# A skipped block of no-operations ahead of three engines' programs, in a sum of reciprocals on one core

## The chip, the cores and the metric

The kernel runs on one core of a Trainium2 chip. The time is the device time of one execution in microseconds (us). The core has five engines with a program each: TensorE (PE, matrix multiply), VectorE (DVE), ScalarE (ACT), GpSimd (POOL) and SyncE (SP, which here issues all DMAs). The engines meet only at semaphores. Sixteen DMA engines move data between the chip's memory (DRAM) and the on-chip memory.

## The reference

```python
def setup_inputs():
    batch, seq, dim = 32, 512, 1024
    return {"x": np.abs(np.random.randn(batch, seq, dim)).astype(np.float32) + 1e-6}

def reference(x):
    return np.sum(1.0 / x, axis=-1).astype(np.float32)
```

The input has 32 x 512 rows of 1024 float32 numbers, 67.1 MB. Of each row the sum of the reciprocals is wanted, 16,384 numbers in all.

## The kernel before

The 16,384 rows lie as 128 partitions of 128 rows each. "Row r" in the kernel means row r of every partition, a tile of 128 x 1024. The last two rows (126 and 127) are worked in two halves each, as rows 126 to 129 of the plan.

Per row the kernel avoids 1024 divisions by pairing the first half a with the second half b: 1/a + 1/b = (a + b) / (a * b). The product a * b goes through ScalarE, which takes its logarithm (scaled by 2^17) and then the exponential of the negative logarithm, so that 1/(a * b) comes out. VectorE multiplies by a + b and sums up in the same instruction, or multiplies a row's both halves by the same reciprocal of the product, which needs no a + b.

The order of all work is written out by hand in the string PLAN (lines 43 to 73), and the same order holds on each engine. A token is a letter, a row, "+n" for n rows at once and "@b" for a place:

- D: SyncE loads the next n rows into `ring`, a buffer of 40 rows (line 187). There are 33 loads, from 7168 KB down to 256 KB. A load waits until the rows that it overwrites are done with.
- P: POOL makes the products a * b of a row into `prod` (line 199). W and V: VectorE makes them (line 220); for V, TensorE has first copied b into a PSUM bank (C, a multiplication by the identity matrix, line 209), for W both halves are read from `ring`.
- S: TensorE forms a + b in a PSUM bank with two multiplications by the identity (line 232).
- L and E: ScalarE's logarithm (line 242) and exponential (line 251). E writes to a PSUM bank where it has an "@".
- R: VectorE's multiplication and sum (line 267), which fills one column of `sums`.
- When the first 114 rows are done, their sums leave in six DMAs (line 289); the rest leaves in one DMA at the end (line 291).

The helper `note` keeps a history of who reads and writes which space (a row of the ring, a slot of `prod`, a PSUM bank). The framework adds a semaphore wait for every dependency that it sees. Where another wait of the same engine already implies a dependency, `note` declares it away with `tc.declare_no_dep`. In the kernel before, a dependency on an earlier instruction of the same engine is passed over ahead of that step:

```python
        for other in needed:
            o_inst, o_engine, o_tick, _, _, o_known = other
            if o_engine == engine:
                continue
            if o_tick <= known.get(o_engine, 0):
                tc.declare_no_dep(inst, o_inst, reason="implied by other waits")
                continue
```

At the head of the programs ScalarE loads its table of functions (line 84) and POOL makes the identity matrix `ident` by `make_identity` (a fill and a select of another file, masks.py:197 and 199). TensorE's first multiplication reads it.

Of the kernel before, what the change touches and what calls it, by code (L numbers as in the profile page):

```python
# [8 lines left out]


@with_exitstack
def kernel(
# [5 lines left out]
    nc = tc.nc  # L18
    f32 = mybir.dt.float32
    P = 128  # L20
# [3 lines left out]
    R = 40  # L24
    NP = 22
    LAST = F - 2
    DONE = 114
    S = float(2**17)

    PLAN = """
        D2 D10 D14 D14 P0+2 C3@3 S2@0 V3 P2 L0+2@0 C11@3 S3@1 E0+2@6 P4+2 V11 L2+2@2 R0 S6@2
        E2+2 R1 P6+2 L4+2@4 R2 R3 E4+2@6 S7@0 P8+2 L6+2@8 R4 S10@1 E6+2 R5 P10 L8+2@10 R6 R7  # L40
        S11@2 E8+2@6 L10+2@6 R8 E10+2 R9 D11 R10 R11 P12+2 C19@3 S14@0 V19 P14+2 L12+2@12
        S15@1 E12+2@6 S18@2 R12 P16+2 L14+2@16 R13 E14+2 R14 P18 L16+2@18 R15 S19@0 E16+2@6
        P20+2 L18+2@14 R16 S22@1 E18+2 R17 D9 P22+2 L20+2@20 R18 R19 E20+2@6 S23@2 P24+2
        L22+2@0 R20 E22+2 R21 L24+2@2 R22 R23 E24+2@6 P26 C27@3 R24 S26@0 P28+2 V27 R25 D7
        L26+2@4 C35@3 E26+2 S27@1 P30+2 V35 L28+2@8 R26 S30@2 R27 E28+2@6 P32+2 L30+2@10 R28
        S31@0 E30+2 R29 P34 L32+2@12 S34@1 R30 R31 E32+2@6 P36+2 S35@0 L34+2@6 R32 E34+2 R33
        D7 P38+2 S38@2 L36+2@16 R34 R35 E36+2@6 S39@1 P40+2 L38+2@18 R36 C43@3 E38+2 R37 D6
        S42@0 P42 L40+2@14 V43 R38 E40+2@6 P44+2 R39 S43@2 L42+2@20 R40 E42+2 S46@1 R41 D3
        P46+2 L44+2@0 R42 R43 E44+2@6 S47@0 P48+2 L46+2@2 R44 S50@2 E46+2 R45 P50 L48+2@4
        R46 C51@3 R47 E48+2@6 S51@1 P52+2 V51 R48 D6 L50+2@8 C59@3 E50+2 R49 P54+2 S54@0  # L50
        L52+2@10 V59 R50 E52+2@6 R51 S55@2 P56+2 L54+2@12 R52 E54+2 S58@1 R53 D5 P58
        L56+2@16 R54 R55 E56+2@6 S59@0 P60+2 L58+2@6 R56 S62@2 E58+2 R57 D4 P62+2 L60+2@14
        R58 R59 E60+2@6 S63@1 P64+2 L62+2@18 R60 S66@0 E62+2 R61 D4 P66 L64+2@20 R62 C67@3
        R63 E64+2@6 P68+2 S67@2 V67 R64 L66+2@0 S70@1 R65 D4 E66+2 P70+2 L68+2@2 R66 R67
        S71@0 E68+2@6 P72+2 L70+2@4 R68 D3 E70+2 R69 D2 C75@3 P74 L72+2@10 S74@2 R70 V75
        P76+2 E72+2@6 R71 S75@1 L74+2@8 R72 D2 E74+2 R73 D2 P80 S78@0 L76+2@12 R74 P81
        L80@16 R75 S79@2 E76+2@6 P78+2 L81@17 R76 D2 S81@1 E80@5 E81 R80 L78+2@6 W82 E78+2
        R81 R77 D1 D1 D1 D1 D1 P88 C85@6 S85@1 R78 P83 L88@18 V85 E88@7 R79 P84 S84@0
        L82+2@14 R88 E82+2@5 P86+2 L84+2@19 R82 D1 E84+2 R83 D1 D1 D1 C90@7 P91 L86+2@0
        S91@2 R85 P93 V90 E86+2@5 R84 P92 S90@1 L90+2@2 R87 L93@21 W89 L92@10 R86 D1 D1 D1  # L60
        D1 E93@7 P94 S97@0 E92@6 R93 E90+2 P97 S94@3 L89@11 R92 E89@7 P95 L97@8 R91 S95@4
        E97 R90 L94+2@4 W96 R97 P101 C99@6 L96@9 R89 E94+2 S100@0 P98 V99 E96@5 L101@12 R95
        P100 S99@1 L98@13 R96 E101@7 L99+2@16 R101 E98@6 P104 C103@5 R94 E99+2 S105@2 R98
        P102 L104@18 V103 E104@7 W105 L102+2@6 R100 P107+2 C106@6 L105@14 R104 E102+2@4
        S108@0 V106 E105 R102 L106+3@19 P109 S107@3 R103 P110 E106+3 R105 S106@4 R99 P111+2
        L109+2@0 R107 S112@1 R108 E109+2@6 R106 L111+2@10 P114 R109 S111@0 E111+2 R110 P113
        L114@15 R111 C115@7 P116 L113@2 R112 E114@6 V115 E113@5 S117@0 P117 R114 L116@3
        L115@8 P118 E116@7 R113 S118@1 E115@6 P119 L117+2@12 R116 E117+2 R115 P120 S120@2
        L119@9 R117 P121 L120@4 S121@3 R118 E119@7 E120 R119 P122 L121@5 S122@0 E121 R120
        P123 L122@18 R121 E122 W124 L123@6 R122 L124@7 W125 S125@1 E123@7 E124@6 R123 P126  # L70
        L125@14 P127 L126@16 S127@0 R124 E125 P128 L127@17 S128@2 E126@7 P129 R125 E127
        S129@3 L128@19 R126 L129@20 E128 R127 E129 R128 R129
    """.split()

    Ln = mybir.ActivationFunctionType.Ln
# [4 lines left out]
    x_v = x.flatten_outer_dims().rearrange("(p f) d -> p f d", p=P)  # L80
    out_v = out.flatten().rearrange("(p f) -> p f", p=P)

    act_sets = list(get_activation_tables(nc.m.arch).keys())
    nc.scalar.add_instruction(  # L84
        mybir.InstLoadActFuncSet(
            name=nc.get_next_instruction_name(),
            act_func_set_id=act_sets.index("natural_log_exp_and_others"),
            ins=[],
            outs=[],
        )  # L90
    )

    pool = ctx.enter_context(tc.tile_pool(name="pool", bufs=1))
    pspool = ctx.enter_context(
        tc.tile_pool(name="pspool", bufs=1, space=bass.MemoryType.PSUM)
# [1 line left out]
    ring = pool.tile([P, R, D], f32)  # L97
# [1 line left out]
    sums = pool.tile([P, F], f32)  # L99
    ident = pool.tile([P, P], f32)  # L100
    ps = pspool.tile([P, 8, H], f32)
    make_identity(nc, ident)

    def parse(tok):
        body, _, b = tok[1:].partition("@")
        r, _, n = body.partition("+")
        return tok[0], int(r), int(n or 1), int(b) if b else None

    ops = [parse(tok) for tok in PLAN]

    pslot = {r + j: b + j for op, r, n, b in ops if op == "L" for j in range(n)}

    def place(r):
        if r < LAST:
# [9 lines left out]
    left = set(range(DONE))  # L124
    bank, copied, halves, summed = {}, {}, set(), set()

    history = {}
    begun = {}
    count = {}

    def note(engine, inst, reads=(), writes=()):
        inst = inst.ins
        known = dict(begun.get(engine, {}))
        before = {}
        for spaces, writing in ((reads, False), (writes, True)):
            for space in spaces:  # L140
                for other in history.get(space, ()):
                    if writing or other[3]:
                        before[other[0].name] = other
        needed = sorted(before.values(), key=lambda o: -o[4])
        for other in needed:
            o_inst, o_engine, o_tick, _, _, o_known = other
            if o_engine == engine:
                continue
            if o_tick <= known.get(o_engine, 0):
                tc.declare_no_dep(inst, o_inst, reason="implied by other waits")  # L150
                continue
            for e, t in o_known.items():
                known[e] = max(known.get(e, 0), t)
            known[o_engine] = max(known.get(o_engine, 0), o_tick)
        count[engine] = count.get(engine, 0) + 1
        begun[engine] = known
        entry = (engine, count[engine])
        if engine == "SP":
            entry = (f"load {count[engine]}", 1)
        for spaces, writing in ((reads, False), (writes, True)):  # L160
            for space in spaces:
                history.setdefault(space, []).append(
                    (inst, *entry, writing, sum(count.values()), known)
                )

    def rows(r, n, h=None):
        spaces = []
# [7 lines left out]
    def slots(r, n):  # L175
        return [("slot", pslot[q]) for q in range(r, r + n)]

    with tc.manual_schedule():
        for op, r, n, b in ops:
            p = pslot.get(r)  # L180
            if op == "D":
                n, r = r, loaded
                while n:
                    q, at, w = place(r)
                    a = q % R
                    m = min(n, R - a, LAST - r) if r < LAST else 1
                    inst = nc.sync.dma_start(  # L187
                        out=ring[:, a : a + m, at : at + 2 * w],
                        in_=x_v[:, q : q + m, at : at + 2 * w],
                    )  # L190
                    note("SP", inst, writes=rows(r, m))
                    r, n = r + m, n - m
                loaded = r
# [34 lines left out]
            elif op == "S":  # L228
                bank[r] = b
                halves.add(r)  # L230
                for h in range(2):
                    inst = nc.tensor.matmul(  # L232
                        ps[:, b, : place(r)[2]],
                        lhsT=ident,
                        rhs=xs(r, h),
                        start=h == 0,
                        stop=h == 1,
                    )
                    note("PE", inst, rows(r, 1, h), [("bank", b)])
            elif op == "L":  # L240
                pg = prod[:, p : p + n, : place(r)[2]]
                inst = nc.scalar.activation(out=pg, in_=pg, func=Ln, scale=S)  # L242
# [1 line left out]
            elif op == "E":  # L244
# [5 lines left out]
                        bank[r + j] = b + j  # L250
                inst = nc.scalar.activation(out=rc, in_=pg, func=Exp, scale=-1.0)  # L251
                if b is None:
                    note("ACT", inst, writes=slots(r, n))
                else:
                    banks = [("bank", b + j) for j in range(n)]
                    note("ACT", inst, slots(r, n), banks)
            elif op == "R":
                q, at, w = place(r)
                other = ps[:, bank[r], :w]
# [2 lines left out]
                else:  # L262
# [16 lines left out]
                    "DVE",  # L279
                    inst,  # L280
                    [("bank", bank[r])],
                    slots(r, 1) if r in halves else rows(r, 1),
                )

                left.discard(r)
                if not left:
                    for c in range(0, DONE, DONE // 6):
                        part = slice(c, min(c + DONE // 6, DONE))
                        nc.sync.dma_start(out=out_v[:, part], in_=sums[:, part])
                    left.add(-1)  # L290
        nc.sync.dma_start(out=out_v[:, DONE:], in_=sums[:, DONE:])


# [28 lines left out]
```

## Time and profile before

| | us |
|---|---|
| three runs | 168.47, 168.10, 167.86 |
| their median | 168.1 |
| span of the profiled execution, first to last instruction | 166.3 |
| SyncE issues the first load | 0.74 |
| first data packet | 1.75 |
| load 0 has landed | 5.6 |
| ScalarE's first logarithm starts | 8.03 |
| TensorE's and VectorE's first work starts | 17.8 and 19.9 |
| last load has landed | 161.3 |
| VectorE's last instruction ends | 164.0 |
| last output has landed | 165.5 |

The span is that of the profiled execution; the runs that were timed are others. A profile names a line, the engine, the operation, and what is written from what ("prod<-ring"). Busy times of the engines overlap. The share of DMA is that of the 16 DMA engines together. A load has landed when all 16 engines have reported the end of their part. "Instruction" among the DMA queues is the fetching of program code; those packets run on the same 16 DMA engines.

### The profile page before, as it was taken

How to read it: one execution, taken by the hardware profiler on the slowest of the kernel's cores; microseconds unless marked ns; L12 is line 12 of the kernel's file. 1: busy time of each engine (PE TensorE's matmuls, PEld its weight loads, DVE VectorE, ACT ScalarE, POOL GpSimd, SP SyncE). 2: the span in 40 equal slices, each digit the busy share in tenths (PEclk: the TensorE clock that was granted, in tenths of full speed). 3: DMA queues.
4: the chain of work that ended last, by engine and by line, in shares of the span. 5: the costliest groups of instructions: out<-in, count | busy, mean ns of one | idle time of the engine just before them, and what ended most of it. 6: DMA issues, size and time to landing. Idle time of an engine off the chain costs nothing.

```text
span 166.3 us, 1348 instructions
## 1 busy us (share of the span) xinstructions
PE 132.5 (80%) x292; PEld 55.2 (33%) x292; DVE 128.3 (77%) x282; ACT 132.3 (80%) x157; POOL 128.2 (77%) x81
## 2 busy tenths in 40 slices
PE   0000799978855999999999999988699979989982
PEld 0000333333312444444343433324234424433351
DVE  0000119885787699898998898989899999999994
ACT  3040073949995899999799999996999999999992
POOL 1500795069995999999999999948977869999860
PEclk9999999999996999999999999999999999999999
DMA  5999999999998989999999999999999999999940
GB/s 189 536 394 394 441 441 441 441 441 441 441 441 349 509 368 446 430 417 438 441 434 434 406 426 446 429 424 424 414 437 437 414 410 428 410 409 410 400 139 4
DMA packets 5768, 67.26 MB, mean 404 GB/s; under 512 B 1536, under 2 KB 1536, under 8 KB 3200
## 3 DMA queue, kind: packets, MB, share of 16 engines
q1 hardware_dynamic: 5760, 67.18, 95.6%
q8 instruction: 2, 0.03, 0.1%
q14 instruction: 6, 0.05, 0.1%
HBM read 67.11 MB, written 0.07 MB: 404 GB/s over the span
## 4 chain that ended last, share of the span: by engine, by line
DMA 57%; PE 18%; ACT 8%; DVE 6%; POOL 6%; issue 3%; SPq 1%; ACTq 0%; POOLq 0%; DVEq 0%
DMA ring<-in_x_dram 57%; PE ps L232 15%; POOL prod L199 6%; ACT prod L242 4%; PE ps L209 3%; ACT ps L251 2%; DVE ring L267 2%; DVE prod L267 2%; ACT prod L251 2%; DVE prod L220 1%; SPq L187 1%; DVE sums L267 0%; ACTq L242 0%; POOLq L199 0%; DVEq L317 0%
## 5 line engine op out<-in xcount | busy, mean ns | idle before, releaser
L199 POOL TENSOR_TENSOR prod<-ring 128x1024 f32<-128x1024 f32 (+2 forms) x75 | 127.5, 1727 | 33.5 <-DMA ring<-in_x_dram 27.1
L232 PE MATMUL ps<-ring,ident 128*128 128x512 f32 (+1 forms) x260 | 116.9, 596 | 5.2 <-DVE sums L267 4.5
L242 ACT ACTIVATE prod<-prod 128x1024 f32<-128x1024 f32 (+2 forms) x78 | 68.5, 892 | 24.9 <-DVE prod L220 14.3
L267 DVE CUSTOM_DVE_ANT_1 ring<-ring,ps 128x1024 f32<-128x1024 f32 (+1 forms) x65 | 76.4, 1208 | 8.9 <-ACT ps L251 8.7
L232 PEld LDWEIGHTS ps<-ring,ident 128*128 128x128 f32 x260 | 49.2, 193 | 71.7 <-issue 51.6
L267 DVE CUSTOM_DVE_ANT_0 prod<-prod,ps 128x512 f32<-128x512 f32 (+1 forms) x63 | 40.9, 677 | 0.4 <-PE ps L232 0.4
L209 PE MATMUL ps<-ring,ident 128*128 128x512 f32 x32 | 19.3, 689 | 25.7 <-DMA ring<-in_x_dram 24.0
L251 ACT ACTIVATE ps<-prod 128x1024 f32<-128x1024 f32 (+2 forms) x41 | 34.1, 838 | 4.5 <-DVE sums L267 3.7
L251 ACT ACTIVATE prod<-prod 128x1024 f32<-128x1024 f32 (+3 forms) x37 | 34.4, 931 | 0.9
L220 DVE TENSOR_TENSOR prod<-ring,ps 128x512 f32<-128x512 f32 x16 | 10.9, 684 | 26.3 <-PE ps L209 26.3
L209 PEld LDWEIGHTS ps<-ring,ident 128*128 128x128 f32 x32 | 6.0, 213 | 36.0 <-issue 21.4
L267 DVE DVE_READ_ACCUMULATOR2_ANT sums<- 128x1 f32 x130 | 10.7, 82 | 0.0
L220 DVE TENSOR_TENSOR prod<-ring 128x512 f32<-128x512 f32 x6 | 4.1, 688 | 0.1
L84 ACT ACT_TABLE_LOAD x1 | 1.3, 1283 | 0.7 <-PEq L306 0.7
L267 DVE CUSTOM_DVE_ANT_0 prod<-prod,ps,sums 128x256 f32<-128x256 f32 x2 | 0.9, 475 | 0.0
masks.py:197 POOL MEMSET ident<- 128x128 f32 x1 | 0.2, 204 | 0.3 <-POOLq L306 0.3
masks.py:199 POOL TENSOR_SCALAR_AFFINE_SELECT ident<-ident 128x128 f32<-128x128 f32 x1 | 0.3, 292 | 0.1
L306 POOL MEMSET const-float32-0.0<- 128x1 f32 x1 | 0.1, 98 | 0.2 <-issue 0.2
L306 POOL MEMSET const-bfloat16-1.0<- 128x1 bf16 x1 | 0.1, 101 | 0.0
L306 POOL MEMSET const-uint8-127<- 128x1 uint8 x1 | 0.1, 101 | 0.0
L306 POOL MEMSET const-float32-1.0<- 128x1 f32 x1 | 0.1, 98 | 0.0
## 6 DMA issues: line engine op xcount, KB each, us to landing
ring<-in_x_dram SPq DMA_DIRECT2D x2, 7168.0 KB, 41.2
ring<-in_x_dram SPq DMA_DIRECT2D x2, 3584.0 KB, 29.3
ring<-in_x_dram SPq DMA_DIRECT2D x2, 3072.0 KB, 31.9
ring<-in_x_dram SPq DMA_DIRECT2D x3, 2048.0 KB, 34.0
ring<-in_x_dram SPq DMA_DIRECT2D x1, 5632.0 KB, 30.3
ring<-in_x_dram SPq DMA_DIRECT2D x5, 1024.0 KB, 31.8
ring<-in_x_dram SPq DMA_DIRECT2D x1, 5120.0 KB, 16.5
ring<-in_x_dram SPq DMA_DIRECT2D x1, 4608.0 KB, 30.7
```

What stands on the lines that cost most here:

```text
L84: nc.scalar.add_instruction(mybir.InstLoadActFuncSet(name=nc.get_next_instruction_name(), act_func_set_id=act_sets.index("natural_log_exp_ ...
L187: inst = nc.sync.dma_start(out=ring[:, a : a + m, at : at + 2 * w], in_=x_v[:, q : q + m, at : at + 2 * w],)
L199: inst = nc.gpsimd.tensor_tensor(out=prod[:, p : p + m, :w], in0=ring[:, a : a + m, at : at + w], in1=ring[:, a : a + m, at + w : at + 2 * w],
L209: inst = nc.tensor.matmul(ps[:, b, : place(r)[2]], lhsT=ident, rhs=xs(r, 1), start=True, stop=True,)
L220: inst = nc.vector.tensor_tensor(out=prod[:, p, :w], in0=xs(r, 0), in1=in1, op=mult)
L232: inst = nc.tensor.matmul(ps[:, b, : place(r)[2]], lhsT=ident, rhs=xs(r, h), start=h == 0, stop=h == 1,)
L242: inst = nc.scalar.activation(out=pg, in_=pg, func=Ln, scale=S)
L251: inst = nc.scalar.activation(out=rc, in_=pg, func=Exp, scale=-1.0)
L267: inst = nc.vector.tensor_tensor_reduce(out=row, in0=row, in1=other, scale=S, scalar=total if q in summed else 0.0, op0=mult, op1=add, acc ...
L306: nc = _bacc.Bacc("TRN2", target_bir_lowering=False, num_devices=1)
```

## The change

Three things change.

First, ahead of the work of TensorE, VectorE and ScalarE there now stands a section that sets a register to 0 and runs 176, 56 or 48 no-operations if it equals 1. It does not, so a branch goes past them. The section is a critical one, as the framework calls it: the three stand one after the other, VectorE's waits for TensorE's and ScalarE's for VectorE's. All five programs are thereby cut into more blocks, with a branch from each to the next: SyncE and POOL have three more branches each. ScalarE's table load, POOL's fill of the identity and the first load are put behind the sections in their own engines' order; they wait for no semaphore for that.

Second, `note` now looks at same-engine dependencies too, so that those implied by other waits are declared away. The built program has 28 semaphore instructions in VectorE's body instead of 42, and 21 in POOL's instead of 33. R's entry in `note` also names the column of `sums` that it writes.

Third, the identity matrix is made by the same two POOL instructions in the kernel itself, instead of by the helper.

The tokens of PLAN are the same 497 in the same order, and each engine's instructions stand in the same order. New letters A and Z, and a mark "!", are understood but not used.

```diff
+    PADS = (('tensor', 176), ('vector', 56), ('scalar', 48))
...
         for other in needed:
             o_inst, o_engine, o_tick, _, _, o_known = other
-            if o_engine == engine:
-                continue
             if o_tick <= known.get(o_engine, 0):
                 tc.declare_no_dep(inst, o_inst, reason="implied by other waits")
+                continue
+            if o_engine == engine:
                 continue
...
+    skips = []
+    for engine, pad in PADS:
+        engine = getattr(nc, engine)
+        with tc.tile_critical() as skip:
+            zero = engine.to_reg(0)
+            with engine.If_eq(zero, 1):
+                for _ in range(pad):
+                    engine.nop(hint="idle", nofuse=True)
+        skips.append(skip)
+
+    def behind(inst):
+        for skip in skips:
+            tc.add_manual_dep(
+                inst.ins,
+                skip.name,
+                mybir.DependencyInfo(
+                    mybir.DependencyClass.NoSync,
+                    mybir.DependencyReason.SCHED_ONLY,
+                ),
+            )
+
+    act_sets = list(get_activation_tables(nc.m.arch).keys())
+    table = nc.scalar.add_instruction(
...
+    behind(table)
 
     with tc.manual_schedule():
-        for op, r, n, b in ops:
+        behind(nc.gpsimd.memset(ident, 0.0))
+        nc.gpsimd.affine_select(
+            out=ident,
+            in_=ident,
...
+        for op, r, n, b, held in ops:
...
+                    if r == 0:
+                        behind(inst)
                     note("SP", inst, writes=rows(r, m))
...
-                    slots(r, 1) if r in halves else rows(r, 1),
+                    (slots(r, 1) if r in halves else rows(r, 1)) + [("sum", q)],
```

## The prediction

> **What bounds the kernel now.** I read the page first, then the chain of waits, then the DMA queues by window, then the timelines of ScalarE and VectorE near the landings that they wait for.
>
> ```profile
> span 166.3 us, 1348 instructions
> PE 132.5 (80%) x292; PEld 55.2 (33%) x292; DVE 128.3 (77%) x282; ACT 132.3 (80%) x157; POOL 128.2 (77%) x81
> DMA  5999999999998989999999999999999999999940
> q1 hardware_dynamic: 5760, 67.18, 95.6%
> q8 instruction: 2, 0.03, 0.1%
> q14 instruction: 6, 0.05, 0.1%
> ...
> DMA 57%; PE 18%; ACT 8%; DVE 6%; POOL 6%; issue 3%; SPq 1%; ACTq 0%; POOLq 0%; DVEq 0%
> ```
>
> The 16 DMA engines are full from the second slice to the 38th, and the chain that ended last is DMA for 57%. Cut into 2 us pieces, the packets of the data queue cover 0.98 to 1.04 of 16 engines from 2 to 158 us: the input stream never pauses. Each load is cut evenly over the 16 engines (8 partitions each), so a load has landed when its slowest engine is through, and whatever else one engine carries makes it late for good. The two lines "instruction" are such extra work: the fetching of program code, 2 packets of 16 KB and 6 of 8 KB.
>
> The trace's landing events show what they cost. Load 3 (the fourth) ends on all 16 engines within 0.38 us (51.18 to 51.56). Then a code packet of 8 KB starts at 52.42, and load 4's last engine is 0.94 behind its first; after the 16 KB packet at 69.64, load 5 shows 1.63; after 8 KB at 78.18 a third engine stands at 0.69; after 8 KB at 109.44 and 111.23, load 10 has 1.97 (110.75 to 112.72); after 16 KB at 140.84 a further engine stands at 1.7. At load 28 (156.65 to 158.67) the spread is 2.03, with engines at 2.03, 1.79, 1.70, 0.78, 0.76 and the other eleven under 0.39. In the packet records a fetch takes its own 0.3 us (8 KB) or 1.0 to 1.1 us (16 KB), and the data packet behind it on the same engine is longer by 0.36 to 0.66: 0.95 us each for the fetches at 52.42 and 111.23, 0.7 for those at 78.18 and 109.44, 1.5 for the 16 KB ones. The fetches at 52.42 and 111.23 hit the same DMA engine (a packet ends on it 4 ns after each starts, the next nearest is 10 ns off or more), the two of 16 KB two different ones.
>
> Who waits for the late engine is in the timelines (start, us, instruction, and the idle time before it with its releaser), of ScalarE and then of VectorE:
>
> ```profile
> 111.76 1.06 ACT L251 ACTIVATE prod<-prod 128x1024 f32<-128x1024 f32 x1
> 114.16 0.63 ACT L242 ACTIVATE prod<-prod 128x512 f32<-128x512 f32 x1 [1.34 <-POOL prod L199]
> ...
> 157.37 0.69 DVE L220 TENSOR_TENSOR prod<-ring 128x512 f32<-128x512 f32 x1
> 157.97 0.68 DVE L267 CUSTOM_DVE_ANT_0 prod<-prod,ps 128x512 f32<-128x512 f32 x1
> 158.58 0.08 DVE L267 DVE_READ_ACCUMULATOR2_ANT sums<- 128x1 f32 x1
> 158.69 0.69 DVE L220 TENSOR_TENSOR prod<-ring 128x512 f32<-128x512 f32 x1
> ```
>
> ScalarE's 1.34 us end with a POOL product that waited for load 10 (112.72). VectorE's W124 and W125 start 0.02 us after loads 27 and 28 have landed (157.34, 158.67); from W125 on VectorE has no gap to its last instruction at 164.0, and 2.3 us of output and end barrier follow. So the end hangs on the slowest DMA engine's landing of loads 27 and 28, with VectorE close behind: between 142 and 158.7 it idles only 0.6 us in all.
>
> **The change part by part.** *Head.* TensorE, VectorE and ScalarE run their branch one after the other (each waits for the one before), SyncE and POOL pass 3 more branches each, and the first load is issued behind SyncE's. No trace row is a lone branch. SyncE's gap from a semaphore row to its DMA is 0.066 us over one branch (0.671 to 0.737) and 0.047 without (35.080 to 35.127): one costs 0.02, and at most the whole 0.066. Three: 0.06 to 0.2; I take 0.1, as the measured difference is the nearer row. It is on the path, since the stream never pauses. The Trainium skill (Advanced Engine Details and Errata, Control Flow Timing) gives about 51 ns for a branch, 0.15 us for three; no row here shows a branch alone. ScalarE's table load (1.28 us, now at 0.73) comes after all three sections. Each has some 10 instructions outside the no-ops, by the sequencer rows of 17 to 51 ns at most 0.5 us each, so it ends by 3.6; ScalarE first works at 8.03. If that cover went, ScalarE's first pair (2.1 us) could still start at 18.5, since it then sits idle 10.53 us until 20.68. TensorE and VectorE first work at 17.8 and 19.9. Cost 0.1.
>
> *Waits removed.* Same-engine waits that others imply: 14 semaphore instructions less on VectorE, 12 on POOL. VectorE's take 0.021 us each, and in the trace the instruction behind them starts within 4 ns of where one without a wait would: the sequencer is ahead, and the running operation (0.68 us or more) hides them. Bounds: 0 and 14 x 0.021 = 0.3 us. POOL's gaps in the chain of waits are 0.05 to 0.09 ("issue" at 137.20 and 139.66): 0 to 12 x 0.09 = 1.1 us, but POOL idles 33.5 us, 27.1 of it for DMA. I take 0 for both.
>
> *Code moved.* The no-ops are not executed but lie in the program: with what is around them TensorE's code grows by 186 instructions ahead of its first matmul, VectorE's by 67, ScalarE's by 61. A code fetch comes when a program passes a certain place. VectorE stands at its instruction 62 to 67 (waits counted, from the span's start) at 52.4 and at 190 to 192 at 111.2, 128 apart: its places are 64, 192, 320. TensorE (two instructions a matmul) is 256 apart: its queue runs some 64 ahead, which puts the places near 243 and 499, the second at most 500, the wait at which it stands until 142.15. Fetch packets start 2 to 2.6 us after. ScalarE fits 78.18 (instruction 66 to 68) and 162.98 (196 to 200). Moved by the insertions, in the old numbers: VectorE at the skip itself (some 1.5 us, fetch at about 3.5), near 130 (84.1 us, fetch 86) and near 264 with the waits removed (142, fetch 144); TensorE at 57 (fetch 22), 313 (the wait at 87.07 lets it run, fetch 91), 569 (behind the wait at 158.70, fetch 161, when the last load is in); ScalarE at about 5 (fetch by 23) and 133 (fetch 129). Between the first and the last load that is VectorE 3 instead of 2, TensorE 2 as before but earlier, ScalarE 2 instead of 1.
>
> What does it do to the slowest engine? The TensorE pair costs 1.5 each on two engines, wherever in time: no gain. ScalarE's engine comes to 1.4: under 2.03. VectorE's engine is the slowest now, at 2 x 0.95. Its third fetch is a page further on: on another engine the spread stays 2.0; on the same engine it becomes 2.9. The head fetch at 3.5 falls among the first packets (from 1.75 on), so it costs up to 0.95; if it is done before the first data, 0. I take the spread at loads 27 and 28 as unchanged, because TensorE's two consecutive pages went to two engines: the bounds are -0.3 (VectorE's engine falls below TensorE's 1.7) and +0.95. The early fetches make loads 1 to 3 up to 1.5 us later, and ScalarE, which waits for them, too; it has 0.83 + 0.29 + 1.34 = 2.46 us idle between 54.5 and 114.2 to give that back before load 10 sets it again.
>
> The Trainium skill (Runtime: NRT & Kernel Launch, Instruction fetch mechanics) says that crossing a 16 KiB boundary is "one DMA tail-bump, mostly hidden". The landing spread, 0.38 before and 2.03 after, does not agree for this DMA-bound kernel. By the page the sum would be the head's 0.1 alone and the slower rival below would fall.
>
> *Sum.* 166.3 + 0.1 + 0 + 0 = 166.4 us span. The shown runs' median of 168.1 lies 1.8 above the profiled span (entry and exit around it); with it 168.2.
>
> **The rivals.** *Slower: the third VectorE fetch sits on the same DMA engine.* Its place is the engine of 52.42 and 111.23, its price 0.95, and it decides once the head fetch comes after 1.75 and the one near 144 hits that engine: loads 27 and 28 land at 158.3 and 159.6, and VectorE's gapless tail follows. 168.1 + 0.95 + 0.1 = 169.15. For it: two fetches in a row did hit one engine. Against: TensorE's two did not.
>
> *Faster: lower spread and cheaper waits.* The head fetch is free, VectorE's engine ends under TensorE's (-0.3), load 10 lands 0.3 earlier into ScalarE's 1.34 gap, and the waits give 0.3 on VectorE and 0.2 of POOL's 1.1 where it sets the chain (137 to 147): 168.1 - 0.8 + 0.1 = 167.4. Against: the 0.6 us that VectorE can still save after 142, and its waits' starts within 4 ns.
>
> *It doesn't do what it says:* the no-ops are run. By sequencer rows (TensorE's 51 ns, VectorE's 21, ScalarE's 17) 9.0 + 1.2 + 0.8 = 11 us, one after the other: the table load ends at about 13, before 18.5. Time as in the forecast, 168.2.
>
> **How the numbers follow.** Three runs spread 0.6 us; below 0.3% (0.5 us) I call it no change. Forecast 168.2 with 0.34 (own range 167.7 to 168.6), no-ops run 0.04, slower rival 0.34, faster rival 0.28. So same 0.38, slower 0.34, faster 0.28. The range 167.2 to 169.4 takes in both rivals and leaves out their tails, some 0.2.
>
> **What would show it.** The table load ends by 4 us, the first load is issued 0.06 to 0.2 later, instruction packets near 3.5, 22, 86, 91, 129 and 144, spread at load 28 about 2.0 (2.9 for the slower rival, 1.7 for the faster), ScalarE's start at 54.5 later by about 1.5, and its gap before 114 shorter by what is left of that. Wrong would make it: a code fetch that stops an engine in the middle, or fetches that keep to other places than every 128 or 256 instructions.

## The result and the profile after

The changed kernel is slower by about 1%: 169.39 us (median of seven executions, 169.26 to 171.73) against 168.1 (seven, 167.86 to 168.75) on the same chip, a ratio of 1.010 with a 95% interval of 1.0051 to 1.0149. Its executions fall into two groups, five at 169.26 to 169.41 and two at 171.04 and 171.73, called the dear ones below, and the profile was taken of the 171.73 one. A ratio leaves out executions more than 1.5% above the fastest of their kernel, which here are none, so that 1.010 averages both groups; below, where it leaves too few for an interval, the times are listed one by one.

From the page of the changed kernel: span, busy times, DMA share in 40 slices, DMA queues (packets, MB, share of 16 engines), the chain that ended last, and from the groups the W products (busy, mean ns).

```profile
span 169.9 us, 1348 instructions
PE 133.0 (78%) x292; PEld 55.3 (33%) x292; DVE 130.8 (77%) x282; ACT 132.3 (78%) x157; POOL 130.6 (77%) x81
...
DMA  5999999999999999999999999999999999999700
...
q1 hardware_dynamic: 5760, 67.18, 93.6%
q8 instruction: 3, 0.05, 0.1%
q14 instruction: 6, 0.05, 0.1%
...
DVE 34%; DMA 20%; PE 17%; ACT 14%; issue 6%; POOL 4%; another core or an unknown queue 2%; SPq 0%; DVEq 0%; ACTq 0%
...
L248 DVE TENSOR_TENSOR prod<-ring 128x512 f32<-128x512 f32 x6 | 7.1, 1188 | 0.0
```

The engines do the same work; one 16 KB code packet more is fetched (q8, 3 instead of 2). Two things stand out. VectorE and POOL are each busy 2.4 to 2.5 us longer (before: 128.3 and 128.2) with the same instructions; of VectorE's, the six W products alone take 7.1 us instead of 4.1. And the chain that ended last is VectorE's (34%) where it was DMA's (57%). The W products on the page of the kernel before:

```profile
L220 DVE TENSOR_TENSOR prod<-ring 128x512 f32<-128x512 f32 x6 | 4.1, 688 | 0.1
```

The same kernel profiled again gave an execution of the other group, 169.44 us. The same lines of its page:

```profile
span 167.7 us, 1348 instructions
...
PEclk9999999975999999999999999999999999999999
...
q8 instruction: 3, 0.05, 0.1%
...
DMA 63%; DVE 12%; PE 11%; ACT 7%; issue 3%; another core or an unknown queue 1%; SPq 1%; ACTq 0%; DVEq 0%
...
L248 DVE TENSOR_TENSOR prod<-ring 128x512 f32<-128x512 f32 x6 | 4.2, 708 | 0.1
```

Here W costs 4.2 us, nearly as before, and the chain is DMA's again, yet the time is 1.2 us above the kernel before. So two costs must be told apart: one of about 1.2 us that every execution pays, and one of about 2 us that only some pay.

The landings by the trace's events, last engine of a load, with its lag behind the load's first engine in brackets:

| load | before | after, 171.73 us | after, 169.44 us |
|---|---|---|---|
| 2 | 34.62 | 36.00 (1.95) | 36.17 |
| 3 | 51.56 (0.38) | 52.95 (1.90) | 53.11 |
| 10 | 112.72 (1.97) | 112.80 | 112.85 |
| 28 | 158.67 (2.03) | 159.46 (2.73) | 159.75 (3.16) |
| VectorE's last end | 164.03 | 167.39 | 165.12 |

In the 169.44 us execution VectorE ends 1.09 us later than before, and load 28 lands 1.08 later: that is the first cost. In the 171.73 us execution load 28 is 0.79 late, but VectorE 3.36.

The head of the changed kernel, in its timeline, of SyncE and then of ScalarE (start, us, instruction, idle time before it with its releaser):

```profile
0.74 2.06 SPq L213 DMA_DIRECT2D ring<-in_x_dram  x4
...
3.82 1.28 ACT L184 ACT_TABLE_LOAD   x1 [3.82 <-ACTq L165]
7.88 1.06 ACT L270 ACTIVATE prod<-prod 128x1024 f32<-128x1024 f32 x1 [2.78 <-POOL prod L227]
```

The first load is issued at 0.74, as before. ScalarE's table load waits for the three sections until 3.82 and ends at 5.10, 2.78 us before the first logarithm at 7.88. The no-operations were skipped: run, they would have kept the table load to about 13 by the prediction's estimate.

### The profile page after: what moved, and what is told of

Read it like the earlier page. It is cut to its first block, busy times and chain, and to the rows that moved or that the text cites. A ratio compares the mean times of both kernels' runs of the same rounds, so it can differ in the third digit from the quotient of the medians.

```text
span 169.9 us, 1348 instructions
## 1 busy us (share of the span) xinstructions
PE 133.0 (78%) x292; PEld 55.3 (33%) x292; DVE 130.8 (77%) x282; ACT 132.3 (78%) x157; POOL 130.6 (77%) x81
## 4 chain that ended last, share of the span: by engine, by line
DVE 34%; DMA 20%; PE 17%; ACT 14%; issue 6%; POOL 4%; another core or an unknown queue 2%; SPq 0%; DVEq 0%; ACTq 0%
DMA ring<-in_x_dram 20%; DVE ring L314 18%; PE ps L260 15%; DVE prod L314 10%; ACT prod L270 7%; DVE prod L248 6%; POOL prod L227 4%; ACT ps L279 4%; ACT prod L279 3%; PE ps L237 3%; DVE sums L314 1%; SPq L213 0%; DVEq L363 0%; ACTq L270 0%
## 5 line engine op out<-in xcount | busy, mean ns | idle before, releaser
L227 POOL TENSOR_TENSOR prod<-ring 128x1024 f32<-128x1024 f32 (+2 forms) x75 | 129.9, 1763 | 32.8 <-DMA ring<-in_x_dram 32.7
L237 PE MATMUL ps<-ring,ident 128*128 128x512 f32 x32 | 19.8, 705 | 24.8 <-DMA ring<-in_x_dram 24.0
L248 DVE TENSOR_TENSOR prod<-ring 128x512 f32<-128x512 f32 x6 | 7.1, 1188 | 0.0
```

Source lines behind the costliest of these rows:

```text
L227: inst = nc.gpsimd.tensor_tensor(out=prod[:, p : p + m, :w], in0=ring[:, a : a + m, at : at + w], in1=ring[:, a : a + m, at + w : at + 2 * w],
L237: inst = nc.tensor.matmul(ps[:, b, : place(r)[2]], lhsT=ident, rhs=xs(r, 1), start=True, stop=True,)
L248: inst = nc.vector.tensor_tensor(out=prod[:, p, :w], in0=xs(r, 0), in1=in1, op=mult)
```

## The experiments

Theories, by the letters that the expectations use. A: every code fetch of VectorE hits one and the same DMA engine, which the end waits for; three instead of two make it 0.95 us later. B: the cost or gain is in the waits that were declared away. C and D are two halves of a chain for the dearer executions: code fetches brought forward make loads 2 and 3 late, so that VectorE works later (C), and VectorE's W products, which read both halves from `ring`, then run beside POOL's products and stretch both (D).

The sections are switched by the one line PADS, the waits by `note`; unless said otherwise the rest is the changed kernel.

### Sections away, one at a time

All sections away; what stays is the new rule for waits and the identity made in the kernel:

```diff
-    PADS = (('tensor', 176), ('vector', 56), ('scalar', 48))
+    PADS = ()
```

> The changed kernel without the three skipped sections; the waits declared away and the rest of the change stay. Theory A (the code fetches count: three VectorE fetches on one DMA engine while loads run make it 0.7 us later than before): VectorE's places are back at 64, 192 and 320, so two of its fetches lie in the load stream, the spread of load 28's landing is 2.0 us, time 168.1 (167.8 to 168.5). Theory B (the removed waits cost time): 169.4, as after. Theory C (loads 2 and 3 late by 1.4 us shift VectorE's W products onto POOL's products): loads 2 and 3 are on time, 168.1.

168.45 us (ten, 168.30 to 168.88) against 168.27, ratio 1.0013 (1.0003 to 1.0022). Load 28 lands at 158.71 with a spread of 2.10, VectorE ends at 164.07: the kernel before. The removed waits gain nothing, and what all else outside the sections costs is at most 0.4 us. B falls.

VectorE's section alone, `PADS = (('vector', 56),)`:

> Only VectorE's section of 56. Theory A: VectorE's fetches near 4 to 6, 82 and 149, all on one DMA engine, spread at load 28 about 2.7, time 168.8 to 169.2. Theory B: 169.4. Theory C: load 3 late by 0.6 at most instead of 1.4, W products stay apart from POOL's, 168.1 to 168.4.

168.99 to 169.28 us (four), ratio 1.0047 (1.0030 to 1.0064). VectorE's fetches come at 6.59, 87.86 and 146.22; load 28 lands at 159.83 with a spread of 3.06 us instead of 2.03. VectorE near loads 27 and 28 in this kernel's timeline:

```profile
157.78 0.68 DVE L314 CUSTOM_DVE_ANT_0 prod<-prod,ps 128x512 f32<-128x512 f32 x1
158.38 0.08 DVE L314 DVE_READ_ACCUMULATOR2_ANT sums<- 128x1 f32 x1
158.56 0.69 DVE L248 TENSOR_TENSOR prod<-ring 128x512 f32<-128x512 f32 x1
159.17 0.68 DVE L314 CUSTOM_DVE_ANT_0 prod<-prod,ps 128x512 f32<-128x512 f32 x1
159.78 0.08 DVE L314 DVE_READ_ACCUMULATOR2_ANT sums<- 128x1 f32 x1
159.86 0.69 DVE L248 TENSOR_TENSOR prod<-ring 128x512 f32<-128x512 f32 x1
```

W124 and W125 start at 158.56 and 159.86, 0.03 us behind load 28's landing in the second case; before they started at 157.37 and 158.69. The end moves with the slowest engine: VectorE ends at 165.20, 1.17 later than before.

The lags of load 28's sixteen parts behind the first of them show where the third fetch went. Before, the last five stood at 0.76, 0.78, 1.70, 1.79 and 2.03 us; here they stand at 0.64, 0.80, 1.73, 1.73 and 3.05, and the other eleven under 0.3. Only the slowest engine has become later, by 1.0 us, and no other took up a fetch. That is A. A section of VectorE too short to move a fetch was not run; that the fetch and not the section costs rests on these landings.

TensorE's section alone, `PADS = (('tensor', 176),)`:

> Only TensorE's section of 176. Theory A: TensorE's fetches near 23, 85 and 155 on three DMA engines, VectorE's two as before, spread at load 28 2.0, time 168.1 (to 168.5). Theory B: 169.4. Theory C: loads 2 and 3 late by about 1.4 as in the changed kernel, W products on POOL's, 169 to 169.4.

168.44, 171.08, 171.76 and 171.80 us. Fetches of TensorE at 21.4, 84.85 and 154.43. In the profiled execution (171.08) load 28 lands at 158.73 with a spread of 2.04, as before, yet VectorE ends at 166.79 and the W products take 6.5 us (mean 1084 ns). So there is a second cost, without A, and it came with the moved TensorE fetch in three of four executions. It is larger than theory C had it (169 to 169.4).

The changed kernel as it is, once more:

> The changed kernel once more, for a profile of one of its usual executions (169.3). Theory A: spread of load 28 at 2.7, W products of VectorE mostly at their plain 0.69 us. Theory C: W products stretched in the usual executions too, by about 1 us in sum or more. Time 169.3.

169.44, 169.64, 171.11 and 171.28 us, ratio 1.0143 (1.0095 to 1.0192); its profile is the second one of the section above. The two groups belong to the kernel, not to one batch.

ScalarE's section alone, `PADS = (('scalar', 48),)`:

> ScalarE's section of 48 alone: fetches near 4 to 8 and 130, 0.7 each on one engine that stays under the slowest (2.0 at load 28). Theory A: 168.2 to 168.5. Loads 1 to 3 late by 0.3 at most; theory D: no execution near 171.

168.56 us (ten, 168.36 to 168.98 and one of 171.17), ratio 1.0023 (1.0012 to 1.0033), some 0.2 us above the kernel without sections; the two intervals overlap, so this is not shown to be a cost.

### Is it the number of VectorE's fetches or their place?

```diff
-    PADS = (('tensor', 176), ('vector', 56), ('scalar', 48))
+    PADS = (('vector', 120),)
```

> VectorE's section alone with 120 no-operations: VectorE's code grows by 131, so its fetches in the stream fall where they do without a section (near 52 and 112, the next past the load stream), but the skip itself passes one more place: a fetch near 6. Theory A (their number counts, not their place): three fetches on one engine, spread at load 28 about 3.0, time 169.0 as e2. If only the late fetch near 146 of e2 counts: spread 2.0, 168.3.

169.16 to 169.75 us (four), ratio 1.0077 (1.0060 to 1.0094). The fetches come at 4.79, 53.31 and about 117.5, elsewhere than with 56 no-operations, and the spread at load 28 is again 2.98. Three fetches cost it at both placings, so their number counts, and a late place is not needed.

### What stretches the W products

The two profiles of the changed kernel show where the dearer execution loses its time. VectorE's W82 (row 82's product) in the 171.73 us execution, in the timeline of VectorE and then of POOL:

```profile
112.03 1.22 DVE L314 CUSTOM_DVE_ANT_1 ring<-ring,ps 128x1024 f32<-128x1024 f32 x1
113.17 0.08 DVE L314 DVE_READ_ACCUMULATOR2_ANT sums<- 128x1 f32 x1
113.17 1.59 DVE L248 TENSOR_TENSOR prod<-ring 128x512 f32<-128x512 f32 x1
114.68 0.67 DVE L314 CUSTOM_DVE_ANT_0 prod<-prod,ps 128x512 f32<-128x512 f32 x1
...
112.94 4.19 POOL L227 TENSOR_TENSOR prod<-ring 128x512 f32<-128x512 f32 x3 [2.04 <-DMA ring<-in_x_dram]
```

and in the 169.44 us execution:

```profile
112.08 0.69 DVE L248 TENSOR_TENSOR prod<-ring 128x512 f32<-128x512 f32 x1
112.69 0.68 DVE L314 CUSTOM_DVE_ANT_0 prod<-prod,ps 128x512 f32<-128x512 f32 x1
...
112.98 3.75 POOL L227 TENSOR_TENSOR prod<-ring 128x512 f32<-128x512 f32 x3 [1.90 <-DMA ring<-in_x_dram]
```

and in the kernel before:

```profile
111.51 0.69 DVE L220 TENSOR_TENSOR prod<-ring 128x512 f32<-128x512 f32 x1
...
112.85 6.07 POOL L199 TENSOR_TENSOR prod<-ring 128x512 f32<-128x512 f32 x4 [2.79 <-DVE sums L267]
```

POOL starts at nearly the same moment in all three, 0.13 to 0.14 us after load 10 has landed (the last view names VectorE as the releaser, but load 10 landed at 112.72 there). Where W82 is done by then (112.08; before 111.51) it takes 0.69 us; where it starts 0.23 us after POOL (113.17) it takes 1.59, and POOL's three products take 4.19 instead of 3.75 us. The next W products go the same way: 1137, 1569, 958 and 1193 ns instead of 681 to 693 before (W89 816 and the others 679 to 693 in the 169.44 us execution), and single POOL products of this size up to 1.73 us instead of 1.28. The other products of VectorE on the same line, whose second operand is in PSUM, keep to 676 to 689 ns. The Trainium skill (SBUF — State Buffer, Who interferes with whom) says that a VectorE instruction with two inputs in SBUF contends with a GpSimd instruction that reads SBUF, that the ports which the two share are an exclusive lock, and that the order of issue decides who blocks. The trace agrees: W82 starts second and ends at 114.76, 0.60 us after POOL's next product started at 114.16, as if it had waited for the first to end. In the profiles with TensorE's section alone, with 64 no-operations and with four fills, all below, the same distance is 0.59 to 0.60 us. One stretched product alone costs little: W89 took 1.10 us in the kernel without any section, at 168.43 us.

Why it starts late is in ScalarE's and TensorE's timelines. W82 stands in VectorE's order behind work on rows whose reciprocals come from ScalarE, and ScalarE was late by 1.39 us at 54.5 and 1.63 at 79.8 (in the 169.44 us execution by 1.05 and 0.56), because load 3 was. Attempts to cut this chain that missed are told first.

Four W products read the second operand from PSUM instead, copied there by TensorE; with TensorE's section alone, and without sections:

```diff
-        L78+2@6 W82 E78+2 ...
+        L78+2@6 C82@3 V82 E78+2 ...
...
-        ... L93@21 W89 L92@10 ...
+        ... L93@21 C89@3 V89 L92@10 ...
...
-        R90 L94+2@4 W96 R97 ...
+        R90 L94+2@4 C96@1 V96 R97 ...
...
-        ... E104@7 W105 L102+2@6 ...
+        ... E104@7 C105@5 V105 L102+2@6 ...
```

> TensorE's section alone, as in e3, but the products of rows 82, 89, 96 and 105 are made from a copy of b in PSUM (C and V) instead of from two halves in the ring (W). Theory D (TensorE's early code fetch makes loads 2 and 3 late, VectorE's W products then run against POOL's products and both are stretched): no stretched products, no execution near 171.5, all within 168.2 to 168.9. Theory A alone (spread) and a theory that TensorE's third fetch at 154 makes the 171.5: executions near 171.5 stay.

> No section, and the same four products from PSUM copies. Theory D: nothing to gain but W89's stretch of 0.4 us in e1; 168.0 to 168.5, against 168.45 of e1. It is the base for e5.

172.03 to 172.13 us with the section (ratio 1.0233, 1.0216 to 1.0250) and 172.04 to 172.10 without (1.0232, 1.0215 to 1.0249). The edit itself costs some 3.7 us (1.0232 against 1.0013 without it): VectorE now waits for TensorE's copies, between 105 and 145 us four waits of 4.9 us in all, the longest 1.5. The pair says nothing on D.

TensorE's fetch moved, `PADS = (('tensor', 64),)`, meant to come after load 3:

> TensorE's section alone with 64 no-operations instead of 176. TensorE's first fetch then falls behind load 3 (near 54 us instead of 21 to 23), the second near 124. Theory D: loads 2 and 3 land on time (34.6 and 51.6), no execution near 171.5, 168.2 to 168.6. A theory that the section itself (the branch, the code before it) makes the 171.5: it stays.

171.43 to 172.40 us (four), ratio 1.0215 (1.0194 to 1.0236). The fetch came at 50.95, not at 54, and hit load 3 itself, which landed at 53.04 with a spread of 2.00. The placing missed, but the run shows the chain: load 3 late by 1.48, ScalarE by 1.48 and 2.36, W products 7.13 us in sum; all four executions are dear.

With 24 no-operations, `PADS = (('tensor', 24),)`, the fetch misses loads 2 and 3:

> TensorE's section alone with 24 no-operations: its first fetch comes near 62 to 64 us, well behind load 3. Theory D: loads 2 and 3 on time (34.6, 51.6), W products apart from POOL's, 168.2 to 168.6. If a section by itself costs: more than that.

168.55 us (ten, 168.36 to 168.74), ratio 1.0016 (1.0006 to 1.0026). The fetch came at 62.67, loads 2 and 3 landed on time, and none of ten executions is near 171. So it is the place of TensorE's fetch, not its section, that makes the second cost frequent. It also comes, seldom, where TensorE's fetch was not moved: in one of ten executions with ScalarE's section alone, and in 3 of 19 of the kernel before in one batch.

W82 moved earlier in the order, with TensorE's section alone and then in the changed kernel:

```diff
-        ... E80@5 E81 R80
-        L78+2@6 W82 E78+2 ...
+        ... E80@5 E81 W82 R80 L78+2@6 E78+2 ...
```

> TensorE's section of 176 alone, as e3, with one token moved: VectorE makes the product of row 82 (W82) one sum (R80, 1.14 us) earlier. Theory D (loads 2 and 3 late, so that W82 runs into POOL's products behind load 10's landing at 112.7 and every later W with it): W82 at about 112.0 instead of 113.2 ends before POOL starts, W products in sum 4.1 to 4.6 us instead of 6.5, no execution near 171.5, all 168.2 to 168.8. If something else makes the 171.5, executions near it stay.

> The changed kernel with W82 one sum earlier. Theories A and D together: what is left is VectorE's third fetch, spread at load 28 2.7 to 3.1, all executions 169.0 to 169.5, none near 171.

168.44, 171.03, 171.04 and 172.53 us with TensorE's section (in this batch the 3 of 19 executions of the kernel before stood at 171.6 to 172.1), and 169.19 to 169.58 in the changed kernel (1.0069, 1.0049 to 1.0088). The two disagree: in the first the dear executions stayed, so W82 at its old place is not needed to start it; only the 168.44 us execution was profiled, and which product met POOL in the others is not on record. In the second none of four was dear, where four of eleven were without the edit; with four executions that can be chance.

### Late work without a late fetch, and W82 away

Two changes test the chain in a cleaner way. The first makes VectorE late by its own hand, in the kernel without sections: fills of an unused tile ahead of V27, two and then four (0.65 us apart). Results and loads stay as they are.

```diff
+    scratch = pool.tile([P, H], f32)
...
-        ... P28+2 V27 R25 ...
+        ... P28+2 K0+4 V27 R25 ...
...
+            elif op == "K":
+                for _ in range(n):
+                    nc.vector.memset(scratch, 0.0)
```

> No section (as e1), and VectorE fills a scratch tile twice (128 x 512, some 0.5 us each) just ahead of the product of row 27 (V27, 53.7 us), which ScalarE waits for. It delays the compute by about 0.6 us at 54 without any code fetch moved and with loads 2 and 3 on time. Theory D: 0.6 is less than the 1.1 to 1.2 that part W82 and W89 from POOL's products: no execution near 171, 168.3 to 168.8.

> The same with four fills: the compute is some 1.7 us late at 54, as in the profile of the changed kernel (1.6). Theory D (late VectorE work runs its W products against POOL's, and each is stretched): executions at 170.5 to 172, W products 6 us or more in sum instead of 4.1 to 4.6. If the 171 comes from TensorE's code fetches or from late loads as such: 168.3 to 168.8, since ScalarE's idle time before 114 takes the 1.7 in.

Two fills: 168.37 us (ten, 168.14 to 168.65 and one of 171.57), ratio 1.0004 (0.9994 to 1.0014); ScalarE is 0.79 to 0.85 late in the profile (168.65 us), and nine of ten executions lose nothing. Four fills: 168.25, 170.88, 171.56 and 172.19 us; ScalarE is 2.09 late at 54.5 and 2.67 at 79.8, more than was planned. From the page and then from VectorE's timeline of the kernel with four:

```profile
span 170.5 us, 1326 instructions
...
L249 DVE TENSOR_TENSOR prod<-ring 128x512 f32<-128x512 f32 x6 | 6.9, 1143 | 0.0
```

```profile
55.46 0.48 DVE L259 MEMSET scratch<- 128x512 f32 x1 [0.17 <-DVE scratch L259]
55.87 0.63 DVE L249 TENSOR_TENSOR prod<-ring,ps 128x512 f32<-128x512 f32 x1
...
114.19 1.34 DVE L249 TENSOR_TENSOR prod<-ring 128x512 f32<-128x512 f32 x1
```

No section moves a fetch, and loads 2 and 3 land at 34.74 and 51.67, on time. So lateness can bring the second cost without a moved fetch and without a late load: in the profile W82 starts at 114.19 and the W products take 6.9 us, and three of four executions are at 170.9 to 172.2. The fourth had the same fills and is not dear, and it was not profiled, so the fills alone do not decide it.

The second takes W82 off VectorE and gives it to POOL, without sections and with TensorE's section:

```diff
-        L78+2@6 W82 E78+2 ...
+        P82 L78+2@6 E78+2 ...
```

> No section (as e1), and row 82's product goes from VectorE (W82) to POOL (P82), into the 2.4 to 2.8 us in which POOL waits for load 10. VectorE has 0.6 us less to do from 111 on, but the end hangs on loads 27 and 28 as well: 167.9 to 168.5, against 168.45.

> TensorE's section of 176 (as e3) with row 82's product on POOL. Theory D: the first product that meets POOL is gone and VectorE is 0.6 us earlier at W89; executions near 171 become fewer or end, W products in sum 3.4 to 4.5 us without W82. If lateness is not the cause: 3 of 4 near 171.5 as in e3 and e9.

Without sections 168.49 us (ten, 168.09 to 168.77), ratio 1.0012 (1.0003 to 1.0022): no gain by itself. With TensorE's section 168.47 (ten, 168.27 to 168.77), ratio 1.0011 (1.0002 to 1.0021), where the same section without the edit gave three of four at 171.08 to 171.80. The pages of TensorE's section alone, and then with the edit:

```profile
span 169.1 us, 1329 instructions
...
L248 DVE TENSOR_TENSOR prod<-ring 128x512 f32<-128x512 f32 x6 | 6.5, 1084 | 0.0
```

```profile
span 166.7 us, 1329 instructions
...
L248 DVE TENSOR_TENSOR prod<-ring 128x512 f32<-128x512 f32 x5 | 3.5, 703 | 0.1
```

The five W products that are left take 703 ns on average, and no execution of ten is dear, where six of eight were with W82 on VectorE at its old place or one sum earlier. With that product on POOL the second cost is gone. The times show this; the profile shows no dear execution avoided, as ScalarE was only 0.50 us late at 79.8 in it.

No version here is faster than the kernel before.

## Why the prediction was wrong

The forecast was no change, 168.2 us. The measured 169.39 lies at the upper end of its range, and for the cost that every execution pays the mechanism is that of its slower rival, which gave 169.15. That the median lies inside the range, by 0.01 us, is luck: five of the seven executions happened not to be dear, and of the next four the median is 170.37. No rival had the dear executions.

*The step that failed: "I take the spread at loads 27 and 28 as unchanged, because TensorE's two consecutive pages went to two engines".* VectorE's third page (the piece of program that one fetch brings) went to the engine of its first two. Load 28's spread became 2.73 and 3.16 in the two profiles, against 2.9 for the rival and 2.03 for the forecast. In VectorE's section alone this was 1.0 us of spread, 1.17 of the profiled end, and 0.8 us of the median. The evidence for the other way was in the prediction: the two VectorE fetches of the kernel before had hit one engine. It was set against one pair of another engine's pages of 16 KB, whose engines say nothing of VectorE's 8 KB pages. The Trainium skill's "mostly hidden" (Runtime: NRT & Kernel Launch, Instruction fetch mechanics) did not hold in this kernel, whose data never pause: with VectorE's section alone, which adds one fetch of 8 KB between first and last load, it is 0.47% slower.

*A term that was not in the sum: the lateness of loads 1 to 3.* The prediction saw it (up to 1.5 us; measured 0.50, 1.38 and 1.39) and gave it back in ScalarE's idle time "before load 10 sets it again". ScalarE does give it back (in the 171.73 us execution it is 1.63 us late at 79.8 and 0.23 at 114.2); VectorE's W products lose their place beside POOL's ahead of that. POOL's start near 112.9 is set by load 10, and before the change W82 starts 1.34 us ahead of it (111.51 to 112.85). In the profiles W82 kept its 0.69 us where it was up to 0.86 us late (two fills, and 120 no-operations on VectorE), and took 1.34 to 1.70 where it was 1.66 to 2.68 late, with some 2.4 to 3 us of W time lost in all; no profile lies in between. With W82 on POOL no execution was dear. What goes with the dear executions stands near load 3, in the timelines of TensorE, first of the 171.73 us execution and then of the 169.44 us one:

```profile
53.00 2.07 PE L237 MATMUL ps<-ring,ident 128*128 128x512 f32 x2 [2.71 <-DMA ring<-in_x_dram]
```

```profile
53.15 1.12 PE L237 MATMUL ps<-ring,ident 128*128 128x512 f32 x2 [2.50 <-DMA ring<-in_x_dram]
```

The two copies that VectorE's V products wait for take 2.07 us instead of 1.12: TensorE's granted clock is 0.5 there from 52.91 to 56.33, while in the other execution such a stretch lies at 35.5 to 42.3 and is over. ScalarE's timeline of the 171.73 us execution shows who pays:

```profile
55.89 1.06 ACT L270 ACTIVATE prod<-prod 128x1024 f32<-128x1024 f32 x1 [2.45 <-DVE prod L248]
```

In the profiles compared, a late load 3 with a half-clock stretch right behind it went with 1.6 us or more of lateness at 79.8 and with stretched W products (the 171.73 us execution, TensorE's section alone, 64 no-operations); a stretch that came earlier went with about 0.5 and none. The mean granted clocks of the executions go the same way. Apart from the two kernels with PSUM copies, 163 executions have one on record, those of the kernel before included, and 22 of them are at 170.88 us or more. All 22 have a mean granted clock of 0.99 or less, as one such stretch makes it; of the 36 at 0.998 or more none is dear, and the 7 at 0.965 or less all are. That is an association: no run set the clock, so whether it selects the dear executions stays open, as does which product besides W82 can start it.

*Head.* Its 0.1 us did not come: SyncE's gap from its semaphore row to the first load is 0.066 us as before, and the profile has no row for its branches. The table load ended at 5.10 and not "by 3.6", still hidden: the three sections took 3.1 us together, where 0.5 us each had been allowed.

*Waits removed: 0* was right. Without sections the ratio is 1.0013, on the side of a loss. VectorE had even less to save after 142 than the 0.6 us of the prediction: from there to 158.7 it is busy for 16.48 of 16.70 us.

*Code moved.* The fetches came near their forecast places, in both the places of 128 and of 256 instructions: VectorE at 6.26, 82.26 and 149.04 (forecast 3.5, 86, 144), TensorE at 23.51, 85.14 and 154.67 (22, 91, 161), ScalarE at 7.71 and 131.59 (by 23, and 129). TensorE's third came before the last load was in, not behind it. One reading of the kernel before was wrong: the fetch at 162.98 was put down to ScalarE. Without sections, where VectorE has 14 instructions fewer, it is gone and one at 157.65 stays; with ScalarE's section alone there is none at either place. So ScalarE's second fetch was that at 157.74, and the one at 162.98, behind the last load, was VectorE's third.

*The sum, as the runs have it,* for an undisturbed execution: waits and identity 0.2 us (ratio 1.0013), VectorE's section 0.6 on top (1.0047 less 1.0013), ScalarE's 0.2 (1.0023 less 1.0013), TensorE's, where no product collides, 0 to 0.1 (1.0016 with 24 no-operations, against 1.0013): 1.0 of the 1.2 us. The terms come from different batches, and the small ones of ScalarE and TensorE lie within the intervals. The remaining 0.2 is not assigned. The dear executions pay some 2 us more.

## What to carry to other kernels

In a kernel whose input stream never pauses, count the code pages that each engine crosses between the first and last load, skipped instructions included, and add them up by DMA engine: a page that falls on the engine that is already last can be paid nearly in full (here 0.8 us in the median for 1.0 us of spread). Where VectorE and POOL both read SBUF, look at how many tenths of a microsecond keep their products apart, because a delay that later waits would absorb can push them onto each other first. A change that only delays a stage early can be tried by itself with a few fills, which tells a late load from what the lateness does.

## What the runs showed of the hardware

- Code that is jumped over is still fetched by place: 56 skipped no-operations on VectorE brought a third page into the stream, and each of its pages of 8 KB made one DMA engine later by some 0.9 to 1.1 us. In every profile with three of VectorE's pages between the first and the last load the spread at load 28 was 2.73 to 3.24, as it must be if all three hit one engine, whether the third came at 117 or at 149; with two it was 1.94 to 2.29.
- A VectorE product with both operands in SBUF took 0.68 to 0.69 us alone and up to 1.70 beside a POOL product, which itself went from 1.28 to 1.73; with an operand in PSUM it never took more than 0.69.
- The clock granted to TensorE fell to 0.5 in stretches of 3.41 us or twice that, one or two of 3.41 us in most of the profiled executions, at times that differ between executions of one kernel (35.85 and 52.91 in one, 35.5 to 42.3 in another).
